# Token-side sums of an MLP block scheme in eight steps, and the second product's operands in the pairs' slots

## The chip, the cores and the metric

One core of a Trainium2 chip runs the whole kernel. The metric is the device time of one execution in microseconds; the time before is the median of three runs. Engines are called PE (matmul), DVE (VectorE), ACT (ScalarE) and SP, whose queue issues all the DMAs that matter here.

## The reference

One encoder block: a gated delta-rule mixer and a dilated attention mixer, gated, projected and added to x, then an MLP. The change lies in the MLP alone:

```python
    h2 = _rmsnorm(x, ln_mlp_pre[l])
    f = jnp.square(jax.nn.relu(jnp.einsum('bsd,df->bsf', h2, w_ff1[l])))
    f = jnp.einsum('bsf,fd->bsd', f, w_ff2[l])
    x = x + _rmsnorm(f, ln_mlp_post[l])
```

x is 1024 tokens by 1024 channels, w_ff1 1024 x 4096, w_ff2 4096 x 1024, all fp32.

## The kernel before

**Arithmetic.** Every fp32 operand X is split in two fp32r parts: `split` (L85 to L87) casts X to X_hi on ACT and subtracts on DVE, X_lo = X - X_hi. `mm3` (L108 to L112) makes one product of three matmuls, hi x hi, hi x lo, lo x hi. So each weight tile costs an ACT cast and a DVE subtraction before PE can finish with it. A weight tile is loaded to `w_raw` and split to `w_hi`, `w_lo`, with two buffers of each.

**Stages around the change.** `out_norm` writes the normalised, transposed MLP input for one half of the tokens (512) into `h_hi` and `h_lo`. While it does this for half 1, `build` issues plain tiles of the first product (`ff1_tile`) for columns c = 0 to 3 and half 0. Then `mlp` runs:

- `mid_blocks` (L998) adds and subtracts quarter blocks of `h` over the tokens' side: t1, and t2, t3, t4, which are split. It works on two channel pairs c = 0, 1; for each c there are 13 DVE operations of 128 x 1024 and three ACT casts. Temporaries have the tag "mid" (three buffers).
- plain tiles: c = 0 to 3 for half 1, then c = 4 and 5 for both halves. One half tile is 8 x 3 matmuls into one "mm" bank; ACT applies the ReLU (L958), DVE squares (L959), SP stores to `d_f` (L961).
- t1 is split into the place of the lower channel half of `h[1]` (called b12).
- `ff1_pair` (L1028) for c = 6, 8, ... 30: two column tiles at once with seven half-size products in place of eight. Their weight-side sums have the tag "mid"; products 1, 2, 4, 5, 6 take their operands from `x_hi`, `x_lo` (five buffers), products 0 and 3 from `w_hi`, `w_lo`. The last two DMAs of a pair store f1 (L1076) and f0 (L1083).
- both pools, "mid" and "midt" (t2 to t4), are closed, and pool "mlp" opens in their place. `ff2` (L963) makes the second product for each half of the tokens: for each of 32 blocks k it loads 128 rows of `d_f` to `f_raw` (L970), splits them to `f_hi`, `f_lo` (three buffers each), loads and splits 128 rows of `w_ff2`, and issues 24 matmuls into eight PSUM banks. Then it normalises and adds `fx`.

**Order.** The code is traced in the program's order; a planner then puts each engine's instructions into that engine's queue. It prefers work that is earlier in the program among what it holds ready, and gives an instruction its waits for data and for free buffers. On the chip each queue is worked off in order.

Of the kernel before, what the change touches and what calls it, by code (L numbers as in the profile page):

```python
# [10 lines left out]
F = mybir.dt.float32  # L11
R = mybir.dt.float32r
# [5 lines left out]
DM = 1024  # L18
# [52 lines left out]
class Kern:  # L71
# [888 lines left out]
        s = slice(512 * halves[0], 512 * halves[-1] + 512)  # L960
        nc.sync.dma_start(self.d_f[col:col + 128, s], f[:, s])  # L961

    def ff2(self, g, p, tmp):  # L963

        nc, a = self.nc, self.a
        bank = [("acc", 4)] * 4 + [("mm", self.mm_bufs)] * 2 + [("tr", 2)] * 2
        q = [self.pp.tile([128, 512], F, name=t, tag=t, bufs=n) for t, n in bank]
        for k in range(32):
            fr = p.tile([128, 512], F, name="f_raw", tag="f_raw", bufs=3)
            nc.sync.dma_start(fr, self.d_f[128 * k:128 * k + 128, 512 * g:512 * g + 512])  # L970
            W = self.wtile(a["w_ff2"][128 * k:128 * k + 128, :], [128, DM])
            f = [p.tile([128, 512], R, name=n, tag=n, bufs=3) for n in ("f_hi", "f_lo")]
            self.split(*f, fr)
            for t in range(4):
                for n in range(2):
                    self.mm3(q[2 * t + n], [x[:, 128 * t:128 * t + 128] for x in f],
                             [x[:, 512 * n:512 * n + 512] for x in W], k == 0, k == 31)
        xs, ys, sums = [], [], []
        for t in range(4):
            x = p.tile([128, DM], F, name="fx", tag="fx", bufs=4)  # L980
            nc.sync.dma_start(x, self.d_x1[512 * g + 128 * t:512 * g + 128 * t + 128, :])
            y = p.tile([128, DM], F, name="fy", tag="fy", bufs=4)
            ss = tmp.tile([128, 4], F, name="ss4", tag="ss4", bufs=12)
            for n in range(2):
                j = tmp.tile([128, 512], F, name="sj3", tag="ftmp", bufs=4)
                nc.scalar.activation(j, q[2 * t + n], AF.Square, accum_out=ss[:, n:n + 1])
                c = slice(512 * n, 512 * n + 512)
                nc.vector.tensor_tensor(y[:, c], q[2 * t + n], self.g_mlp[:, c], op=OP.mult)
            xs.append(x), ys.append(y), sums.append(ss)
        for t, (x, y, ss) in enumerate(zip(xs, ys, sums)):  # L990
            rows = slice(512 * g + 128 * t, 512 * g + 128 * t + 128)
            r = self.rms_of(tmp, ss[:, 0:2])
            for n in range(2):
                c = slice(512 * n, 512 * n + 512)
                nc.vector.scalar_tensor_tensor(y[:, c], y[:, c], r, x[:, c], op0=OP.mult, op1=OP.add)
                nc.sync.dma_start(a["out"][rows, c], y[:, c])

    def mid_blocks(self, h, pt, p):  # L998

        nc = self.nc  # L1000
        (H0, L0), (H1, L1) = h
        T = [[pt.tile([128, 4, 512], R, name=f"t{n}_{x}") for x in ("hi", "lo")] for n in (2, 3, 4)]
        t1 = p.tile([128, 4, 512], F, name="t1")
        new = lambda: p.tile([128, 2, 512], F, name="mid", tag="mid", bufs=3)
        add = lambda o, x, y: nc.vector.tensor_tensor(o, x, y, op=OP.add)
        sub = lambda o, x, y: nc.vector.tensor_tensor(o, x, y, op=OP.subtract)
        for c in range(2):
            u, v = slice(2 * c, 2 * c + 2), slice(4 + 2 * c, 6 + 2 * c)
            d = new()
            sub(t1[:, u], H1[:, u], H0[:, u])  # L1010
            sub(d, L1[:, u], L0[:, u])
            add(t1[:, u], t1[:, u], d)
            t3, d = new(), new()
            sub(t3, H1[:, v], H1[:, u])
            sub(d, L1[:, v], L1[:, u])
            add(t3, t3, d)
            self.split(T[1][0][:, u], T[1][1][:, u], t3)
            t2 = new()
            sub(t2, H1[:, v], t1[:, u])
            add(t2, t2, L1[:, v])  # L1020
            self.split(T[0][0][:, u], T[0][1][:, u], t2)
            t4 = new()
            sub(t4, H0[:, v], t2)
            add(t4, t4, L0[:, v])
            self.split(T[2][0][:, u], T[2][1][:, u], t4)
        return t1, T

    def ff1_pair(self, c, rhs, pf, p, tmp):  # L1028

# [53 lines left out]
        nc.sync.dma_start(self.d_f[128 * c:128 * c + 128], f0)  # L1083

    def mlp(self, h, pf, tmp):
        with ExitStack() as es:
            p = self.pool("mid", ctx=es)
            pt = self.pool("midt", ctx=es)
            t1, T = self.mid_blocks(h, pt, p)
            for c in range(4):  # L1090
                self.ff1_tile(c, h, (1,), pf)
            for c in range(4, 6):
                self.ff1_tile(c, h, (0, 1), pf)
            b12 = [x[:, 0:4] for x in h[1]]
            self.split(*b12, t1)
            rhs = dict(zip(("t2", "t3", "t4"), T), t1=b12, b11=[x[:, 0:4] for x in h[0]],
                       b21=[x[:, 4:8] for x in h[0]], b22=[x[:, 4:8] for x in h[1]])
            for c in range(6, 32, 2):
                self.ff1_pair(c, rhs, pf, p, tmp)
        p = self.pool("mlp")  # L1100
        self.g_mlp = self.row(p, "ln_mlp_post")
        for g in range(2):
            self.ff2(g, p, tmp)

    def row(self, p, name):
        t = p.tile([128, DM], F, name=name)
# [136 lines left out]
```

## Time and profile before

| | |
|---|---|
| median of 3 runs | 2261.99 us (2260.46 to 2264.52) |
| profiled execution | 2262.11 us, its span 2260.2 us |
| mean granted clock of PE | 0.988 |
| busy: PE, DVE, ACT | 97%, 64%, 34% of the span |
| the MLP's stages | plain tiles with sums to 1644, pairs to 1891, second product to 2248 |

Idle time counts where an engine on the chain that ended last stands still; PE makes 90% of that chain. In a row of a timeline the numbers are start and duration; in square brackets stand the idle time before and what ended it. Matmuls overlap: one of 512 columns lasts 0.39 us by its row and the next starts 0.23 us after it.

### The profile page before, as it was taken

Reading aid. Unit: us, or ns where it says so; the run is one execution under the profiler, and the core shown is the slowest. Engines: PE = TensorE matmul, PEld = TensorE weight load, DVE = VectorE, ACT = ScalarE, POOL = GpSimd, SP = SyncE. Lnnn points to the kernel's source line nnn. Section 1 sums busy time; section 2 is a strip of 40 time slices with the busy share of each in tenths; the row PEclk is TensorE's granted clock in tenths of the full one; section 3 lists DMA queues with packets and bytes.
Section 4 is the critical chain, followed back from the end, with each engine's and each line's share of the span. In section 5 each row is a group of like instructions: output and inputs, shape, how many; then the busy total and the mean of one; then the engine's idle time right before and its main releaser. Section 6 shows DMA issues by size and latency. Waiting matters only on the chain.

```text
span 2260.2 us, 30868 instructions
## 1 busy us (share of the span) xinstructions
PE 2192.2 (97%) x11763; PEld 1856.5 (82%) x11763; DVE 1435.9 (64%) x2538; ACT 779.6 (34%) x1663; POOL 61.4 (3%) x90
## 2 busy tenths in 40 slices
PE   7999999999999999999999999999799998999998
PEld 6887888879778878888888888988588887888886
DVE  5657563999599456777777755567656663335334
ACT  5334343333312323333333322434233332223322
POOL 0211211000000000000000000000000000000000
PEclk9999999999999999999999999999899999999999
DMA  5554755533732665444434257554233335445543
GB/s 176 174 166 136 221 156 158 162 113 102 173 86 71 176 195 159 116 117 117 117 117 117 91 192 249 174 178 142 85 107 112 112 112 181 149 140 173 195 144 107
DMA packets 300603, 326.05 MB, mean 144 GB/s; under 512 B 83012, under 2 KB 238620, under 8 KB 299432
## 3 DMA queue, kind: packets, MB, share of 16 engines
q1 hardware_dynamic: 300456, 324.09, 46.8%
q8 instruction: 92, 1.51, 0.3%
q14 instruction: 55, 0.45, 0.1%
HBM read 237.82 MB, written 89.37 MB: 145 GB/s over the span
## 4 chain that ended last, share of the span: by engine, by line
PE 90%; DVE 5%; ACT 2%; DMA 1%; issue 1%; SPq 0%; DVEq 0%; ACTq 0%
PE mm L112 15%; PE mm L110 15%; PE mm L111 15%; PE acc L1051 9%; PE acc L110 4%; PE acc L111 4%; PE acc L112 4%; PE tr L807 2%; PE gm L110 2%; PE gm L112 2%; PE gm L111 2%; PE ao L585 2%; PE mm L1051 2%; PE tr L110 1%; PE tr L112 1%; PE tr L111 1%
## 5 line engine op out<-in xcount | busy, mean ns | idle before, releaser
L110 PE MATMUL mm<-hT_hi,w_hi 128*128 128x512 f32 x960 | 391.0, 407 | 1.0 <-ACT xpad L335 0.6
L112 PE MATMUL mm<-hT_hi,w_lo 128*128 128x512 f32 x960 | 387.4, 404 | 1.3 <-DVE w_lo L87 1.2
L111 PE MATMUL mm<-hT_lo,w_hi 128*128 128x512 f32 x960 | 388.6, 405 | 0.0
L87 DVE TENSOR_TENSOR w_lo<-w_raw,w_hi 128x1024 fp32r<-128x1024 f32 (+1 forms) x225 | 260.7, 1159 | 148.3 <-ACT w_hi L86 146.4
L86 ACT CAST w_hi<-w_raw 128x1024 fp32r<-128x1024 f32 (+1 forms) x225 | 221.4, 985 | 335.5 <-PE mm L111 195.4
L112 PEld LDWEIGHTS mm<-hT_hi,w_lo 128*128 128x128 f32 x960 | 181.3, 189 | 34.7 <-DVE w_lo L87 3.5
L110 PEld LDWEIGHTS mm<-hT_hi,w_hi 128*128 128x128 f32 x960 | 181.4, 189 | 34.4 <-ACT vs L524 1.3
L111 PEld LDWEIGHTS mm<-hT_lo,w_hi 128*128 128x128 f32 x960 | 181.5, 189 | 31.2 <-issue 0.9
L87 DVE TENSOR_TENSOR f_lo<-f_raw,f_hi 128x512 fp32r<-128x512 f32 x64 | 44.2, 692 | 198.6 <-ACT f_hi L86 198.6
L340 DVE SCALAR_TENSOR_TENSOR cu<-xpad,conv,cu 128x1024 f32<-128x1024 f32 x96 | 125.4, 1307 | 3.3
L86 ACT CAST f_hi<-f_raw 128x512 fp32r<-128x512 f32 x64 | 39.9, 623 | 238.4 <-PE tr L111 225.3
L431 DVE TENSOR_TENSOR XA<-XB 128x62 f32<-128x62 f32 (+30 forms) x124 | 106.1, 856 | 20.5 <-ACT XB L427 17.7
L110 PE MATMUL mm<-w_hi,hT_hi 128*128 128x256 f32 x384 | 108.0, 282 | 0.3 <-ACT V L521 0.3
L434 DVE TENSOR_TENSOR XB<-XB,XA 128x62 f32<-128x62 f32 (+30 forms) x124 | 106.1, 856 | 3.0
L112 PE MATMUL mm<-w_hi,hT_lo 128*128 128x256 f32 x384 | 108.0, 282 | 0.0
L111 PE MATMUL mm<-w_lo,hT_hi 128*128 128x256 f32 x384 | 108.0, 282 | 0.0
L110 PE MATMUL acc<-w_hi,f_hi 128*128 128x512 f32 x256 | 100.8, 394 | 7.2 <-ACT f_hi L86 7.2
L111 PE MATMUL acc<-w_lo,f_hi 128*128 128x512 f32 x256 | 100.6, 393 | 0.0
L112 PE MATMUL acc<-w_hi,f_lo 128*128 128x512 f32 x256 | 100.6, 393 | 0.0
L110 PE MATMUL gm<-hT_hi,w_hi 128*128 128x512 f32 x208 | 83.5, 401 | 0.7 <-ACT bg L652 0.5
L576 ACT ACTIVATE P<-lg,st 128x256 f32<-128x256 f32 (+1 forms) x96 | 45.5, 474 | 109.9 <-DVE st L573 108.0
L112 PE MATMUL gm<-hT_hi,w_lo 128*128 128x512 f32 x208 | 81.9, 394 | 0.0
(336 smaller groups left out, 4932.7 us busy)
## 6 DMA issues: line engine op xcount, KB each, us to landing
w_raw<-in_w_ff SPq DMA_DIRECT2D x100, 512.0 KB
w_raw<-in_w_in SPq DMA_DIRECT2D x85, 512.0 KB
f_raw<-d_f SPq DMA_DIRECT2D x64, 256.0 KB
d_f<-f SPq DMA_DIRECT2D x28, 512.0 KB
d_g<-bg SPq DMA_DIRECT2D x32, 256.0 KB
G<-d_gcb SPq DMA_DIRECT2D x16, 512.0 KB
d_G<-G SPq DMA_DIRECT2D x16, 512.0 KB
E<-d_gcb SPq DMA_DIRECT2D x16, 512.0 KB
```

What stands on the lines that cost most here:

```text
L86: self.nc.scalar.copy(H, src)
L87: self.nc.vector.tensor_tensor(L, src, H, op=OP.subtract)
L110: t.matmul(p, lH, rH, start=first, stop=False)
L111: t.matmul(p, lH, rL, start=False, stop=False)
L112: t.matmul(p, lL, rH, start=False, stop=last)
L340: nc.vector.scalar_tensor_tensor(u, xp[:, t:t + S], cw[:, t:t + 1], u, op0=OP.mult, op1=OP.add)
L431: nc.vector.tensor_tensor(tv, XB[:, 0:j, j:j + 1].to_broadcast([128, j, n]), XB[:, j:j + 1, j + 1:64].to_broadcast([128, j, n]), op=OP.mult)
L434: nc.vector.tensor_tensor(dst, dst, tv, op=OP.add)
L576: nc.scalar.activation(P[:, 0:W], lg[:, 0:W], AF.Exp, bias=nm, scale=-1.0, accum_out=Z)
L585: nc.tensor.matmul(o[:, oc:oc + 128], V[:, kt], PT[:, 128 * n:128 * n + 128], start=n == 0, stop=n == len(keys) - 1)
L807: nc.tensor.matmul(o[:, t], x, y, start=i == 0, stop=i == len(mats) - 1)
L1051: nc.tensor.matmul(bank, X[x][:, k], r[y][:, k], start=start, stop=k == 3 and n == 2, skip_group_check=not first)
```

## The change

Two edits, both in the MLP.

1. `mid_blocks` becomes a generator. It hands out t1 and T first and then stops after each of eight steps (for each c: t1; t3; t2; t4). `mlp` asks for one step after each of the four half-1 tiles, and for two after each of the tiles c = 4 and 5. All operations stay.
2. Pool "mid" stays open to the end. In `ff2`, `f_raw` has the tag "mid", and `f_hi`, `f_lo` have the tags "x_hi", "x_lo" (five buffers). Only "midt" is closed; a pool "end" with the row `ln_mlp_post`, `fx` and `fy` takes its place.

```diff
-    def ff2(self, g, p, tmp):
+    def ff2(self, g, p, pe, tmp):
...
-            fr = p.tile([128, 512], F, name="f_raw", tag="f_raw", bufs=3)
+            fr = p.tile([128, 512], F, name="f_raw", tag="mid", bufs=3)
             nc.sync.dma_start(fr, self.d_f[128 * k:128 * k + 128, 512 * g:512 * g + 512])
             W = self.wtile(a["w_ff2"][128 * k:128 * k + 128, :], [128, DM])
-            f = [p.tile([128, 512], R, name=n, tag=n, bufs=3) for n in ("f_hi", "f_lo")]
+            f = [p.tile([128, 512], R, name=f"f_{n}", tag=f"x_{n}", bufs=5) for n in ("hi", "lo")]
             self.split(*f, fr)
...
-            x = p.tile([128, DM], F, name="fx", tag="fx", bufs=4)
+            x = pe.tile([128, DM], F, name="fx", tag="fx", bufs=4)
...
-            y = p.tile([128, DM], F, name="fy", tag="fy", bufs=4)
+            y = pe.tile([128, DM], F, name="fy", tag="fy", bufs=4)
...
+        yield t1, T
         for c in range(2):
...
             add(t1[:, u], t1[:, u], d)
+            yield
...
             self.split(T[1][0][:, u], T[1][1][:, u], t3)
+            yield
...
             self.split(T[0][0][:, u], T[0][1][:, u], t2)
+            yield
...
             self.split(T[2][0][:, u], T[2][1][:, u], t4)
-        return t1, T
+            yield
...
     def mlp(self, h, pf, tmp):
+        p = self.pool("mid")
         with ExitStack() as es:
-            p = self.pool("mid", ctx=es)
-            pt = self.pool("midt", ctx=es)
-            t1, T = self.mid_blocks(h, pt, p)
+            mid = self.mid_blocks(h, self.pool("midt", ctx=es), p)
+            t1, T = next(mid)
             for c in range(4):
                 self.ff1_tile(c, h, (1,), pf)
+                next(mid)
             for c in range(4, 6):
                 self.ff1_tile(c, h, (0, 1), pf)
+                next(mid), next(mid)
+            for _ in mid:
+                pass
...
-        p = self.pool("mlp")
-        self.g_mlp = self.row(p, "ln_mlp_post")
+        pe = self.pool("end")
+        self.g_mlp = self.row(pe, "ln_mlp_post")
         for g in range(2):
-            self.ff2(g, p, tmp)
+            self.ff2(g, p, pe, tmp)
```

## Rows read from the trace of the kernel before

**Rows 1.** The page, busy time of the engines (share of the span) and instructions

```profile
PE 2192.2 (97%) x11763; PEld 1856.5 (82%) x11763; DVE 1435.9 (64%) x2538; ACT 779.6 (34%) x1663; POOL 61.4 (3%) x90
```

**Rows 2.** Waits of PE, whole span: us in total, times, longest

```profile
PE mm L112 <- DVE w_lo L87: 19.8, 5, 17.9
...
PE acc L110 <- ACT f_hi L86: 7.2, 1, 7.2
```

**Rows 3.** Table by stage: stretch, length, busy by engine, granted clock, DMA share, GB/s

```profile
1580.00:1606.00 26.00, 7.95 (x24) 6.10 (x25) 24.88 (x23) 6.36 (x7) 0.00 (x0) 0.61 0.15 43
...
1893.00:1906.00 13.00, 7.43 (x22) 5.88 (x23) 2.03 (x3) 1.85 (x3) 0.00 (x0) 0.61 0.89 289
```

**Rows 4.** Timeline of PE, 1580 to 1604

```profile
1580.14 0.50 PE L110 MATMUL mm<-h_hi,w_hi 128*128 128x512 f32 x1 [0.95 <-ACT f L958]
1580.48 0.40 PE L111 MATMUL mm<-h_lo,w_hi 128*128 128x512 f32 x1
1598.78 0.79 PE L112 MATMUL mm<-h_hi,w_lo 128*128 128x512 f32 x1 [17.91 <-DVE w_lo L87]
...
1603.55 0.39 PE L111 MATMUL mm<-h_lo,w_hi 128*128 128x512 f32 x1
```

**Rows 5.** Timeline of DVE, 1571 to 1598

```profile
1571.81 1.22 DVE L1006 TENSOR_TENSOR t<-h_hi,h_hi 128x1024 f32<-128x1024 f32 x1
1572.94 0.68 DVE L87 TENSOR_TENSOR h_lo<-tr,h_hi 128x512 fp32r<-128x512 f32 x1
...
1576.47 1.22 DVE L1006 TENSOR_TENSOR mid<-h_hi 128x1024 f32<-128x1024 f32 x1
1577.61 1.22 DVE L1006 TENSOR_TENSOR mid<-h_lo 128x1024 f32<-128x1024 f32 x1
...
1597.51 1.21 DVE L87 TENSOR_TENSOR w_lo<-w_raw,w_hi 128x1024 fp32r<-128x1024 f32 x1
```

**Rows 6.** Timeline of ACT, 1573 to 1623

```profile
1573.15 1.06 ACT L86 CAST w_hi<-w_raw 128x1024 fp32r<-128x1024 f32 x1 [1.31 <-PE mm L111]
...
1579.50 0.59 ACT L958 ACTIVATE f<-mm 128x512 f32<-128x512 f32 x1
...
1617.42 0.59 ACT L958 ACTIVATE f<-mm 128x512 f32<-128x512 f32 x1
...
1622.86 0.59 ACT L958 ACTIVATE f<-mm 128x512 f32<-128x512 f32 x1
```

**Rows 7.** DVE's groups by line, 1571.8 to 1622.8: busy us, mean ns, idle before

```profile
L87 DVE TENSOR_TENSOR t_lo<-mid,t_hi 128x1024 fp32r<-128x1024 f32 x6 | 7.2, 1217 | 1.1 <-ACT t_hi L86 1.1
```

**Rows 8.** Chain that ended last, in order of time, 1892 to 1898

```profile
1892.76 0.33 SPq L1083
1893.13 4.69 DMA f_raw<-d_f
1897.90 0.63 ACT f_hi L86
```

**Rows 9.** Timeline of PE, 1890 to 1904

```profile
1890.98 0.39 PE L1051 MATMUL acc<-h_hi,x_lo 128*128 128x512 f32 x1
1898.57 0.79 PE L110 MATMUL acc<-w_hi,f_hi 128*128 128x512 f32 x1 [7.20 <-ACT f_hi L86]
...
1903.84 0.40 PE L110 MATMUL mm<-w_hi,f_hi 128*128 128x512 f32 x1
```

**Rows 10.** Timelines of ACT and then DVE, 1872 to 1884

```profile
1872.19 0.62 ACT L86 CAST x_hi<-mid 128x512 fp32r<-128x512 f32 x1 [2.09 <-PE acc L1051]
...
1877.81 0.59 ACT L1056 COPY keep<-acc 128x512 f32<-128x512 f32 x1 [1.37 <-PE acc L1051]
...
1883.31 0.69 DVE L1070 TENSOR_TENSOR f<-keep,acc 128x512 f32<-128x512 f32 x1 [6.09 <-PE acc L1051]
```

**Rows 11.** Timeline of ACT, 1629 to 1633

```profile
1629.56 0.62 ACT L86 CAST x_hi<-mid 128x512 fp32r<-128x512 f32 x1 [1.39 <-DVE mid L1037]
...
1632.42 0.62 ACT L86 CAST x_hi<-w_raw 128x512 fp32r<-128x512 f32 x1
```

## The prediction

> **What bounds the kernel now.** The page comes first: TensorE (PE) is busy for 97% of the span [rows 1], so time can only be won where PE stands still or runs slowly. The waits of PE over the whole span are read next. Nearly all of them are far from this change or under a microsecond, but two belong to the MLP, and each is a single long wait: 17.9 us for one `w_lo`, and 7.2 us for one `f_hi` [rows 2]. The table by stage then shows that each wait is followed by slow work: in 1580 to 1606 and in 1893 to 1906 the granted clock averages 0.61 [rows 3], that is, part of these stretches ran at 1.2 GHz, the lower level, after PE had stood idle.
>
> The timelines give the prices. A plain tile takes 5.44 us in the undisturbed stretch (from one evacuation to the next, 1617.42 to 1622.86, [rows 6]), and it has 8 x 3 = 24 matmuls, so the fast step is 5.44 / 24 = 0.227 us.
>
> *First wait.* PE begins tile c = 0 of token half 1, does two matmuls, and stops from 1580.48 to 1598.78 [rows 4]: 18.30 - 0.23 = 18.07 us lost. From 1598.78 to 1603.55 it makes 11 steps in 4.77 us, where fast ones take 2.50: 2.27 us more. Cause: this tile's `w_hi` was cast by 1574.2 [rows 6], but VectorE (DVE) starts its `w_lo` only at 1597.51 [rows 5]. In between DVE works through the sums of `mid_blocks` with hardly a pause, one 1024-wide operation every 1.135 us (1576.47, 1577.61). These sums come earlier in the program than the tile, and DVE prefers them whenever they are ready.
>
> *Second wait.* After the last matmul of the last pair (1890.98) the first matmul of `ff2` starts at 1898.57 [rows 9]: 7.59 - 0.23 = 7.36 us lost. From there to 1903.84 are 12 steps in 5.27 us instead of 2.72: 2.55 us more. The chain of waits names the cause: SP's queue issues the last store of `f` at 1892.76, the first `f_raw` load directly behind it at 1893.13, the load takes 4.69 us, and the cast follows [rows 8]. The load is of rows stored long before; what it waited for is memory, because pool "mlp" lies where the pairs' pool was.
>
> Together: 18.07 + 2.27 + 7.36 + 2.55 = 30.25 us.
>
> **The change part by part.**
>
> *Steps.* No operation is added or removed. The 26 wide DVE operations of `mid_blocks` (13 for each c) and six ScalarE casts keep their number; their place in the program moves behind tiles. Now `w_lo` of the first half-1 tile precedes step 1, that of the second precedes step 2, and so on. What a moved step issues is DVE and ScalarE work only; it has no DMA, so SP's queue is passed by nothing. That DVE is not bound to the program's order is shown by its timeline: the first sum runs at 1571.81, ahead of the `h_lo` at 1572.94 that belongs to the earlier `out_norm` [rows 5]. So I expect ready sums to keep filling DVE's idle time from 1571.8 on, and a ready `w_lo` to be taken at the next free slot, behind one running operation (1.1 us) and whatever DVE hasn't yet done of the steps ahead of it. The worst is c = 5, with steps 5 and 6 ahead (7 operations, 7.9 us, and its own 1.1); but its `w_hi` is ready 9.8 us before its matmuls (two half tiles less a cast).
>
> What hides the sums is 8 half tiles on PE. Without the stall PE reaches the half-1 tiles at 1580.14 - 0.95 = 1579.2 [rows 4] and the pairs at 1579.2 + 8 x 5.44 = 1622.7. From 1571.8 that is 50.9 us. DVE's work in it: 26 sums and 6 `w_lo`, 32 x 1.135 = 36.3; nine squares (two left of half 0, seven of these eight half tiles), one `h_lo` and the first pair's 10 pieces, all 512 wide at 0.605 (0.68 for one [rows 5], less the 0.08 by which successive ones overlap, as 1.22 against 1.135), 20 x 0.605 = 12.1. Sum 48.4 us of 50.9: it fits, with 2.5 us spare. Only one of the pair's ten pieces is needed at its start, so I charge nothing. If that cover were gone, the excess would reappear as a wait at the pairs' start.
>
> Here the Trainium skill speaks against the change: "VectorE: DVE Perf Modes" gives an fp32 two-input operation (N + 151) / 0.96 GHz (section on the TRN2 errata) and says that the next one doesn't start until the pipe is empty (section on the DRAIN). An estimate by that page is 32 x 1.224 + 20 x 0.691 = 53.0 us, 2.1 over, so the time would be up to 2.1 later. The trace agrees with the duration (1.22), but its starts are 1.135 apart; I go by the starts.
>
> The short 0.95 us wait at 1580.14, put down to the evacuation at 1579.50 [rows 4, 6], isn't addressed. It could go or stay, or a wait like it could be added at another boundary: bounds -0.95 and +0.95, value 0.
>
> *Slots.* `f_raw` takes a slot of "mid", `f_hi` and `f_lo` those of "x_hi" and "x_lo", and nothing of ff2's first operands waits for the pairs' pool to close. When are they free? The last split of the last pair is cast at 1872.19, and its `x_lo` ends by 1873.6, so all "mid" slots are free then; the first "x" slot goes with the product whose evacuation starts at 1877.81 [rows 10]. Ahead of the loads in the program stands the row load of `ln_mlp_post`, now in pool "end" on top of "midt": its last reader is the fourth product, ended by 1883.31 [rows 10]. Even if SP puts the `f_raw` load behind that row load, it issues by 1883.7, lands 4.7 later at 1888.4, and `f_hi` (0.67 to the start of PE) is ready at 1889.1, 2.1 us before PE needs it at 1891.2. So the wait and its slow clock vanish: 9.91 us. The four `fx` loads (0.5 MB each) move ahead with "end". They could only delay loads for later k; their cost lies between 0 and the 4.69 of one load [rows 8], and I take 0, since k = 3 is needed three tiles (16 us) later.
>
> Could `ff2` steal slots from the pairs? In the stretch before the first pair, the cast of `x_hi` straight from `w_raw` (fifth in the program's order) runs at 1632.42, after that from `mid` at 1629.56, for which ScalarE idled 1.39 us [rows 11], although the sum in that `mid` reads the same weight tile. That reads as slots handed out in the program's order, so I cost this at nothing.
>
> Sum: the profiled execution took 2262.1 (span 2260.2 and 1.9 around it), within 0.1 of the median of the three runs. 2262.1 - 30.25 = **2231.9**; own range 2229 to 2236 (0.95 either way, the page's 2.1, small waits).
>
> **The rivals.**
>
> *DVE fills up.* Each of the six `t_lo` waits for its cast on ScalarE, and once before DVE idled 1.1 us for it [rows 7]. If all six do, 48.4 + 6.6 = 55.0, that is 4.1 us over; PE then waits and slows (2.27): 2231.9 + 6.4 = 2238.3. Against it: during 1571.8 to 1597 other ready sums nearly always filled such waits. Chance 0.08.
>
> *The loads stay late.* If SP's order puts `f_raw` behind the store of f1 or f0, whose data come from the last pair's squares, the second wait stays in part or whole: 2231.9 + (2.6 + 2.5, from a load issued at 1888.4) = 2237, to 2231.9 + 9.91 = 2241.8. For it: SP takes its queue in order, and [rows 8] show just this line-up. Against it: the loads are ready 10 us before those stores. Chance 0.10.
>
> *The steps don't change DVE's order.* If the order was set by when operations are ready and `w_lo` counts as late, the first stall stays: 2262.1 - 9.9 = 2252.2. Against it: `w_hi` was done at 1574.2. Chance 0.05; for neither part working, 2262, 0.02.
>
> *Slower: the steps stand in DVE's queue in the program's order.* Then at each tile's end comes the evacuation (0.59), the square (0.61), the step (3 operations, 3.4 us, or 4, 4.5) and only then the next `w_lo` (1.13), while PE has 0.45 us of matmuls that don't need it. The first four boundaries cost 5.3 + 6.4 + 5.3 + 5.3, that with seven operations 9.8, the last (six, and a 512-wide `w_lo`) 8.2: 40.3 us, with 2.3 us of slow clock after each 54: 2231.9 + 54 = 2286. It makes the kernel slower once six boundaries lose over 5.0 us each. The engine's queue is first in, first out by the Trainium skill ("TensorE: Matmul & The Clock Gate", row on queue depth), which the late `w_lo` agrees with. Against this rival stands the sum at 1571.81 ahead of earlier work [rows 5]. Chance 0.05.
>
> **How the numbers follow.** Forecast 0.70, rivals as above. Range 2228 to 2242: the forecast's own 2229 to 2236, a microsecond below, and the first two rivals up to 2241.8; together 0.88, and cutting off the second would leave out too much. Two tenths of a per cent (4.5 us) is about what a measurement of this kernel can tell from no change. Faster by more: 0.70 + 0.08 + 0.10 + 0.05 = 0.93. Within: 0.02. Slower: 0.05.
>
> **What would show it.** Right: PE's waits no longer hold the two long rows; the granted clock is 1.00 throughout 1580 to 1630; `w_lo` of the first half-1 tile starts within 2 us of its `w_hi`, with sums spread between later ones; the first `f_raw` is issued before the last pair's stores; `ff2`'s first matmul follows the last pair's within 0.5 us, near 1871. Wrong: a new DVE wait at the start of the pairs or at tile boundaries, idle time of DVE before `t_lo`, or waits within the pairs, which had none.

## The result, and the profile after

The changed kernel takes 2231.13 us (median of four, 2227.34 to 2232.79), the kernel before 2262.89 beside it. The ratio is 0.9858, with a 95% interval of 0.9841 to 0.9875: about 32 us faster. The forecast was 2231.9. The profiled execution took 2232.79, with a span of 2231.0, so the two traces to be compared differ by 29.2 us in span. One later execution of the changed kernel, the profiled one beside the kernel with three buffers for `xr` below, took 9735.5 us; its trace isn't read, and it counts in no ratio.

First the waits of PE from 1500 us to the end (us in total, times, longest). The two long waits of [rows 2] are gone. Of the row for `w_lo` 2.4 us are left, nearly all of it one wait of 2.3 us near 1567 us, and the 0.95 us of [rows 4] is gone too.

```profile
PE mm L112 <- DVE w_lo L87: 2.4, 2, 2.3
PE mm L110 <- ACT w_hi L86: 0.2, 1, 0.2
```

Then the table by stage (length, busy by engine, granted clock, DMA share, GB/s). In 1580 to 1606, where [rows 3] show 7.95 us of PE and 0.61, PE is busy all the time at a clock of 1.00; so it is in 1871 to 1884, which now holds the start of `ff2`. The stage before, 1551 to 1580, holds the wait of 2.3 us and has 0.94.

```profile
1551.00:1580.00 29.00, 26.35 (x120) 20.71 (x119) 24.61 (x45) 14.34 (x32) 0.00 (x0) 0.94 0.61 191
1580.00:1606.00 26.00, 26.00 (x117) 21.52 (x116) 25.97 (x26) 10.67 (x13) 0.00 (x0) 1.00 0.46 142
...
1871.00:1884.00 13.00, 13.00 (x59) 10.78 (x58) 4.07 (x6) 3.97 (x6) 0.00 (x0) 1.00 0.86 289
```

DVE's timeline answers to [rows 5]. The `w_lo` at 1577.60 is that of the first half-1 tile; its `w_hi` was cast from 1575.41 to 1576.46. In [rows 5, 6] the same pair of operations lay 23 us apart. The next `w_lo` follows at 1582.14, after three sums, and so on. The last sums end at 1616.9, and the first pair's pieces at 1622.9.

```profile
1575.81 1.21 DVE L1008 TENSOR_TENSOR mid<-h_lo,h_lo 128x1024 f32<-128x1024 f32 x1
1576.99 0.69 DVE L959 TENSOR_TENSOR f<-f 128x512 f32<-128x512 f32 x1
1577.60 1.22 DVE L87 TENSOR_TENSOR w_lo<-w_raw,w_hi 128x1024 fp32r<-128x1024 f32 x1
1578.73 1.22 DVE L1007 TENSOR_TENSOR t<-t,mid 128x1024 f32<-128x1024 f32 x1
1579.87 1.22 DVE L1008 TENSOR_TENSOR mid<-h_hi 128x1024 f32<-128x1024 f32 x1
1581.00 1.22 DVE L1008 TENSOR_TENSOR mid<-h_lo 128x1024 f32<-128x1024 f32 x1
1582.14 1.22 DVE L87 TENSOR_TENSOR w_lo<-w_raw,w_hi 128x1024 fp32r<-128x1024 f32 x1
...
1615.66 1.22 DVE L87 TENSOR_TENSOR t_lo<-mid,t_hi 128x1024 fp32r<-128x1024 f32 x1
...
1622.21 0.68 DVE L87 TENSOR_TENSOR x_lo<-mid,x_hi 128x512 fp32r<-128x512 f32 x1
1623.78 2.29 DVE L87 TENSOR_TENSOR h_lo<-t,h_hi 128x2048 fp32r<-128x2048 f32 x1 [0.88 <-ACT h_hi L86]
```

At the second place, SP's timeline shows the first `f_raw` load at 1848.74, and loads on both sides of the last pair's stores (1869.11 and 1873.82) where [rows 8] have them behind the last store.

```profile
1848.74 0.32 SPq L970 DMA_DIRECT2D f_raw<-d_f  x1
...
1863.90 0.33 SPq L1118 DMA_DIRECT2D ln_mlp_post<-in_ln_mlp_post  x1
1864.29 0.43 SPq L981 DMA_DIRECT2D fx<-d_x  x1
...
1869.11 0.32 SPq L1082 DMA_DIRECT2D d_f<-f  x1
...
1873.82 0.32 SPq L1089 DMA_DIRECT2D d_f<-f  x1
```

And PE's timeline there, in place of [rows 9]: the first matmul of `ff2` follows the last one of the pairs 0.23 us later, at full speed.

```profile
1871.64 0.39 PE L1057 MATMUL acc<-h_hi,x_lo 128*128 128x512 f32 x1
1871.87 0.39 PE L110 MATMUL acc<-w_hi,f_hi 128*128 128x512 f32 x1
1872.10 0.39 PE L111 MATMUL acc<-w_lo,f_hi 128*128 128x512 f32 x1
```

**Where the 29.2 us went.** Four marks cut both traces (before, then after): the evacuation of the last half-0 tile starts at 1579.50 and 1581.76; the pairs at 1643.69 and 1624.35; `ff2` at 1898.57 and 1871.87; the last matmul at 2249.07 and 2219.80.

| Stretch | before | after | difference | forecast |
|---|---|---|---|---|
| to the end of half 0's tiles | 1579.50 | 1581.76 | +2.26 | 0 |
| half-1 and later plain tiles | 64.19 | 42.59 | -21.60 | -20.34 |
| pairs and the step to `ff2` | 254.88 | 247.52 | -7.36 | -7.36 |
| `ff2` to the last matmul | 350.50 | 347.93 | -2.57 | -2.55 |

The +2.26 lies ahead of the changed code. There, in this execution, a load of x for `out_norm` came late. DVE waited 1.44 us for it, the `w_lo` that a tile needed stood behind its consumers on DVE, and PE stood still for 2.26 us (0.9 in the trace before) and then made six slow steps. DVE's row and then PE's:

```profile
1564.18 1.28 DVE L932 SCALAR_TENSOR_TENSOR xr<-y,r,xr 128x1024 f32<-128x1024 f32 x1 [1.44 <-DMA xr<-in_x]
```

```profile
1567.85 0.79 PE L112 MATMUL mm<-h_hi,w_lo 128*128 128x512 f32 x1 [2.26 <-DVE w_lo L87]
1568.44 0.63 PE L110 MATMUL mm<-h_hi,w_hi 128*128 128x512 f32 x1
1568.87 0.63 PE L111 MATMUL mm<-h_lo,w_hi 128*128 128x512 f32 x1
...
1571.01 0.44 PE L110 MATMUL mm<-h_hi,w_hi 128*128 128x512 f32 x1
```

### The profile page after: what moved, and what is told of

Read it like the earlier page. It is cut to its first block, busy times and chain, and to the rows that moved or that the text cites. A ratio compares the mean times of both kernels' runs of the same rounds, so it can differ in the third digit from the quotient of the medians.

```text
span 2231.0 us, 30874 instructions
## 1 busy us (share of the span) xinstructions
PE 2188.4 (98%) x11763; PEld 1854.1 (83%) x11763; DVE 1433.1 (64%) x2538; ACT 778.6 (35%) x1663; POOL 63.0 (3%) x90
## 4 chain that ended last, share of the span: by engine, by line
PE 89%; DVE 4%; DMA 2%; ACT 2%; issue 1%; SPq 0%; POOL 0%; DVEq 0%; ACTq 0%; POOLq 0%
PE mm L112 15%; PE mm L110 14%; PE mm L111 14%; PE acc L1057 10%; PE acc L110 4%; PE acc L111 4%; PE acc L112 4%; PE gm L110 2%; PE tr L807 2%; PE gm L112 2%; PE gm L111 2%; PE ao L585 2%; PE mm L1057 2%; PE tr L110 1%; PE tr L111 1%; PE tr L112 1%
```

## Experiments

The theory: 20.3 us (with the 0.95 us wait 21.3) come from the steps and 9.9 from the slots, independently; the steps work because DVE prefers what is early in the program among what is ready, and the slots because `f_raw` had waited for memory. The rivals are those of the prediction. Medians stand beside those of the kernel before on the same chip; ratios are to that kernel. Edits are shown against the changed kernel, and three dots mark what is left out of them.

**The changed kernel again.**

> The changed kernel again, beside the others of this group. Theory (two stalls removed: 20.3 us from the steps with their slow clock, 9.9 from the slots): about 31 us under the kernel before, 2228 to 2234. It also tells whether the 2.3 us wait at 1567 us, which the first trace of the changed kernel shows behind a late xr load and a slow clock after it, is there in every execution: if it comes and goes, spans differ by 2 to 5 us with it.

2232.51 us against 2263.91, ratio 0.9863 (0.9845 to 0.9881). In this execution the wait near 1567 us was 0.7 us, with no slow clock (1551 to 1580 at 1.00), so the 2.3 us come and go. Its span is 2230.7 all the same, so a few microseconds come and go in earlier stages too.

**Steps alone.** `ff2` and its pool as before:

```diff
-            fr = p.tile([128, 512], F, name="f_raw", tag="mid", bufs=3)
+            fr = p.tile([128, 512], F, name="f_raw", tag="f_raw", bufs=3)
...
-        pe = self.pool("end")
+        p = self.pool("mlp")
```

> Only the steps; ff2 keeps its own buffers in pool mlp. Theory: the first stall goes (18.07 + 2.27, and the 0.95 at the boundary), the second stays with 7.4 us and its slow clock: 2262.5 - 21 = 2241.5, between 2239 and 2244. Rival (the two edits need each other, or the steps only move the wait to the pairs' start): above 2250.

2240.21 us, ratio 0.9899 (0.9878 to 0.9921). Of the two long waits only the second is left; waits of PE from 1500 us on:

```profile
PE acc L110 <- ACT f_hi L86: 6.7, 1, 6.7
PE mm L112 <- DVE w_lo L87: 1.1, 2, 0.9
```

SP's timeline shows that the order of [rows 8] is still there, the load right behind the last store:

```profile
1868.59 0.33 SPq L1118 DMA_DIRECT2D ln_mlp_post<-in_ln_mlp_post  x1
1869.94 0.33 SPq L1089 DMA_DIRECT2D d_f<-f  x1
1870.32 1.94 SPq L970 DMA_DIRECT2D f_raw<-d_f  x3
```

The row load of `ln_mlp_post`, which goes into the same pool as `f_raw`, is issued at 1868.59, as the last matmul of the pairs ends. So, as far as the rows show, the load of `f_raw` waited for memory until about then, and the rest of the 1.7 us up to 1870.32 for its place in SP's queue behind the store. In the trace before the same two loads lie 1.7 us apart too, at 1891.40 and 1893.13.

**Slots alone.** The sums are drawn before the first half-1 tile:

```diff
             t1, T = next(mid)
+            for _ in mid:
+                pass
             for c in range(4):
                 self.ff1_tile(c, h, (1,), pf)
-                next(mid)
...
-                next(mid), next(mid)
-            for _ in mid:
-                pass
```

> Only the slots; all sums come before the half-1 tiles as before. Theory: the second stall goes (7.36 + 2.55), the first stays: 2262.5 - 9.9 = 2252.6, between 2251 and 2255. Rival (loads stay late without the steps): 2262.

2252.78 us, ratio 0.9951 (0.9936 to 0.9966), 0.2 from the expected value. The first wait is back with its old size, and with it the 1.0 us wait for an evacuation:

```profile
PE mm L112 <- DVE w_lo L87: 18.8, 3, 17.9
PE mm L110 <- ACT f L958: 1.0, 1, 1.0
```

The two parts alone give 23.7 and 11.1 us against the common 2263.91, the whole 31.4; the ratios' intervals are wide enough for parts that simply add up (1.0 and 0.5% against 1.4%).

**All sums behind the first half-1 tile.**

```diff
                 self.ff1_tile(c, h, (1,), pf)
-                next(mid)
+                if c == 0:
+                    for _ in mid:
+                        pass
...
-                next(mid), next(mid)
-            for _ in mid:
-                pass
```

> Both edits, but all 26 sums stand behind the first half-1 tile instead of in eight steps. Theory (DVE prefers what comes earlier in the program among what is ready, so the second tile's w_lo waits for the sums): the first stall moves one tile later, from 5 us shorter than before to as long: PE waits 12 to 18 us for w_lo of tile c = 1 and then runs slowly for 2.3 us, 2245 to 2252. Rival (it is enough that the first tile has its weights; the number of steps does nothing): as the changed kernel, 2231.

2250.11 us, ratio 0.9935 (0.9919 to 0.9952). The wait has moved one tile on. PE's timeline, and then DVE's `w_lo` of the second tile, whose `w_hi` was done at 1582.5 (1581.44 and 1.06 on ScalarE):

```profile
1588.52 0.50 PE L110 MATMUL mm<-h_hi,w_hi 128*128 128x512 f32 x1 [1.00 <-ACT f L958]
1603.40 0.80 PE L112 MATMUL mm<-h_hi,w_lo 128*128 128x512 f32 x1 [14.15 <-DVE w_lo L87]
```

```profile
1602.13 1.22 DVE L87 TENSOR_TENSOR w_lo<-w_raw,w_hi 128x1024 fp32r<-128x1024 f32 x1
```

A ready `w_lo` stood 19.6 us behind sums that are earlier in the program. So it isn't enough that the first tile has its weights.

**All sums behind the last plain tile, no steps.**

```diff
                 self.ff1_tile(c, h, (1,), pf)
-                next(mid)
             for c in range(4, 6):
                 self.ff1_tile(c, h, (0, 1), pf)
-                next(mid), next(mid)
             for _ in mid:
                 pass
```

> Both edits, but no steps: all 26 sums stand behind the last plain tile. Theory (what matters is only that a ready w_lo stands ahead of the sums; ready sums fill DVE's idle time wherever they stand): first sum still at about 1572 to 1574 us, no wait of PE, same time as the changed kernel, ratio 0.984 to 0.988. Rival (the spreading itself is needed, since sums that come last are also done last): a wait at the start of the pairs, 5 us or more above the changed kernel.

2233.41 us, ratio 0.9869 (0.9856 to 0.9883): not to be told from the changed kernel. The first sum still starts at 1574.38, before the first half-1 tile, though in the program all sums now stand behind the plain tiles, and the last one ends at 1617.3, about as with the steps:

```profile
1574.38 1.22 DVE L1008 TENSOR_TENSOR t<-h_hi,h_hi 128x1024 f32<-128x1024 f32 x1
...
1616.06 1.23 DVE L87 TENSOR_TENSOR t_lo<-mid,t_hi 128x1024 fp32r<-128x1024 f32 x1
```

So eight steps aren't needed. What counts is that no long block of sums stands ahead of a `w_lo` in the program: all 26 cost 14 to 18 us of waiting, the three or four of a step none. With all sums behind the tiles the planner spreads them by itself.

**`f_raw` in pool "end".**

```diff
-            fr = p.tile([128, 512], F, name="f_raw", tag="mid", bufs=3)
+            fr = pe.tile([128, 512], F, name="f_raw", tag="f_raw", bufs=3)
```

> As the changed kernel, but f_raw has buffers of its own in pool end (on top of midt) instead of the slots of mid. Theory (the load waited for memory, and midt is free 8 us before the end of the last pair): loads are issued at about 1864 instead of 1849, land by 1869, the cast is ready about 2 us before PE needs it: same time, ratio 0.984 to 0.989. Rival (the loads get behind the stores of the last pair or share the DMA engines with the fx loads): PE waits 2 to 7 us for f_hi and then runs slowly, 2236 to 2242.

2232.56 us, ratio 0.9864 (0.985 to 0.9877), no wait at `ff2`. This is the order that the prediction took as its worst case (loads behind the row load). The lines are from SP's, ScalarE's and PE's timelines, a fence each:

```profile
1865.07 0.33 SPq L1118 DMA_DIRECT2D ln_mlp_post<-in_ln_mlp_post  x1
1865.44 1.37 SPq L970 DMA_DIRECT2D f_raw<-d_f  x3
```

```profile
1870.25 1.96 ACT L86 CAST f_hi<-f_raw 128x512 fp32r<-128x512 f32 x3 [1.87 <-DMA f_raw<-d_f]
```

```profile
1873.03 0.39 PE L110 MATMUL acc<-w_hi,f_hi 128*128 128x512 f32 x1
```

From issue to cast are 4.8 us, and with 0.67 for the cast the operand is ready 2.1 us before PE uses it, the very margin of the prediction. So the load needed free memory early, not the slots of "mid" in particular.

**Six and thirteen more sums.** The sums added write to a tile of their own that nothing reads, (3, 3) and (7, 6) for the two c:

```diff
+        spare = pt.tile([128, 2, 512], F, name="spare")
...
+            for _ in range((3, 3)[c]):
+                sub(spare, H1[:, v], H0[:, v])
             sub(t4, H0[:, v], t2)
```

> As the changed kernel, with six more sums of 1024 columns (three in each fourth step of a c), whose results nothing reads. Theory (DVE has 2.5 us spare before the pairs, and 9 of the first pair's 10 pieces, 5.4 us, may come later): 6 x 1.135 = 6.8 us are still covered; 0 to 1 us slower than the changed kernel, no wait of over 1 us at the pairs' start. Rival (DVE is full already, as its timeline without idle time suggests): 7 us and a slow clock, 9 us slower.

> As the changed kernel, with 13 more sums (seven and six), whose results nothing reads. Theory: 14.8 us against 2.5 + 5.4 of cover, so PE waits about 6.9 us in the first pair and then runs slowly for 2.3: 7 to 11 us slower than the changed kernel. Rival (DVE full): 14.8 + 2.3 = 17 us slower. Rival (sums are hidden further on in the pairs, where DVE is 60% busy): nothing.

With six, 2234.55 us, ratio 0.9875 (0.9859 to 0.9891); with thirteen, 2246.03, ratio 0.9928 (0.9914 to 0.9942). PE's waits from 1550 us on, first with six, then with thirteen:

```profile
PE acc L1060 <- DVE x_lo L87: 1.6, 1, 1.6
```

```profile
PE acc L1060 <- ACT x_hi L86: 9.4, 1, 9.4
```

6.8 us of extra work cost 1.6 us of waiting, and 14.8 cost 9.4, 0.8 more at a tile boundary, and then slow steps (in 1630 to 1650 the clock averages 0.74). PE's timeline with thirteen shows both waits:

```profile
1604.06 0.50 PE L112 MATMUL mm<-h_hi,w_lo 128*128 128x512 f32 x1 [0.83 <-DVE w_lo L87]
...
1635.51 0.79 PE L1060 MATMUL acc<-t_hi,x_hi 128*128 128x512 f32 x1 [9.39 <-ACT x_hi L86]
```

So 5.2 and 4.6 us were covered, against 2.5 + 5.4 = 7.9 expected, and both expectations were missed: with six the wait is over the 1 us allowed for, and with thirteen the time is about 14 us above the changed kernel's, not 7 to 11. One thing that was missing is the split of t1, which is earlier in the program than the pair's pieces and takes DVE 2.2 us in the same place; DVE's timeline with thirteen:

```profile
1629.64 1.22 DVE L1008 TENSOR_TENSOR spare<-h_hi,h_hi 128x1024 f32<-128x1024 f32 x1
1630.78 2.28 DVE L87 TENSOR_TENSOR h_lo<-t,h_hi 128x2048 fp32r<-128x2048 f32 x1
1632.98 1.22 DVE L1008 TENSOR_TENSOR spare<-h_hi,h_hi 128x1024 f32<-128x1024 f32 x1
1634.12 0.68 DVE L1046 TENSOR_TENSOR mid<-w_raw 128x512 f32<-128x512 f32 x1
```

That leaves 7.9 - 2.2 = 5.7. With thirteen, the rows give the rest: DVE also makes a tenth square ahead of the first piece (0.6 us), the cast of that piece lies between DVE and PE (0.8 us, from the next start on DVE at 1634.72 to 1635.51), and PE makes two matmuls of the pair before it waits (0.5 us): 5.7 - 0.6 - 0.8 + 0.5 = 4.8. With six, PE waits for the fifth piece and not for the first, after 14 matmuls of the pair, so that its 5.2 us follow from another sum, which isn't worked out here. The rival by which DVE has no room at all (7 and 14.8 us of wait) falls, and so does the one by which the pairs hide everything.

**Three buffers for `xr`,** to look at what is left before the pairs, with the changed kernel beside it:

```diff
-            x = p.tile([128, DM], F, name="xr", tag="xr", bufs=2)
+            x = p.tile([128, DM], F, name="xr", tag="xr", bufs=3)
```

> As the changed kernel, but out_norm has three buffers for xr instead of two, so the third load of x in each half no longer waits for a buffer. Theory (what is left before the pairs is the load of xr: it landed 6.7 us after its issue in the first trace of the changed kernel, w_lo stood behind its consumer on DVE, PE waited 2.3 us and ran slowly for 3 us, but 0.7 us without slow clock in other traces): the wait at 1567 to 1571 goes, 0.7 to 3.5 us faster than the changed kernel, ratio 0.9845 to 0.986. Rival (the wait is the order of DVE's work and not the load): the 0.7 us stay, no difference.

> The changed kernel beside it on the same chip: ratio 0.985 to 0.988, and a look at whether its wait at 1567 to 1571 us is 0.7 or 2.3 us in this execution.

2232.2 us, ratio 0.9859 (0.9844 to 0.9873), against 0.9856 (0.9839 to 0.9872) for the changed kernel: no difference. What the wait was in the changed kernel beside it isn't known. With three buffers PE's longest wait from 1500 us on is still 0.7 us for a `w_lo`, although no load of xr is late here: the tile's `w_hi` was done at 1564.5, and its `w_lo` starts only at 1567.91, behind operations of `out_norm`. So the 0.7 us come from the order of DVE's work, as the rival had it. Whether a third buffer would prevent the 2.3 us, which showed in two traces of these kernels (the first of the changed kernel, and that with all sums behind the first tile), stays open: the late load didn't occur where it could have been compared.

## Why the prediction was right, point by point

**The two prices.** Both stalls were read as start-to-start distances plus the slow steps behind them, and the table of four marks gives them back: 7.36 against 7.36 for the wait at `ff2`, 2.57 against 2.55 for its slow clock. For the first stall it is 21.60 against 20.34. That the median lies within 0.8 us of the forecast is in part luck: the executions scatter over 5 us, and in the profiled one the 1.26 us gained beyond the price at the first stall and the 2.26 us lost ahead of it partly cancel.

**The short wait at the boundary (value 0, bounds of 0.95 either way).** It went, and with it 0.95 of the 1.26 us by which the first stall's gain exceeds its price. The runs show more than the prediction saw: the wait is in every kernel in which PE waits over 14 us for a `w_lo` (before, slots alone, all sums behind the first tile) and in none of the others. It went with the stall; why the bank was given out so that the tile waited isn't shown.

**The steps.** That DVE takes ready sums early and a ready `w_lo` before later sums is what its timeline shows. The prediction let each step follow a tile, as the change does; the run with all sums behind the plain tiles shows that the eight steps aren't needed for it, only that the block doesn't stand ahead of the `w_lo`.

**The cover.** 48.4 us of DVE work were reckoned into 50.9. In the trace after DVE works from 1573.46 to 1622.9 with under 0.3 us of idle time. It began 1.7 us later than reckoned because of the late x load, and so did the pairs (1624.35 against 1622.7). The sum by starts 1.135 and 0.605 us apart holds: 32 operations of 1024 columns and 21 of 512 (ten pieces, nine squares, two `h_lo`) give 49.0 us for these 49.4. By the Trainium skill ("VectorE: DVE Perf Modes", the sections on the errata and on the DRAIN), the same work is an estimated 32 x 1.224 + 21 x 0.691 = 53.7 us; the measurement decides for the starts. In its section on the DRAIN the Trainium skill adds that an operation which isn't held starts earlier, which the estimate in the prediction had left out; the rows agree, with starts 1.135 us apart at 1.22 us long. The prediction's own slip is the split of t1: its 2.2 us on DVE come at the pairs' start and belong into the sum of what must be done there. By the two runs with more sums the change has about 5 us of cover (5.2 and 4.6) rather than the 7.9 that follow from the prediction's terms. Since the change adds no work, the slip cost nothing.

**The slots.** Right in time, and in mechanism but for one part: the prediction laid the load's wait to memory alone, and the last 1.4 us or so of it were its place behind the store in SP's queue (1.7 us after the row load, where 0.4 us lie between the two with `f_raw` in "end"). Free memory removed both, since the load then went ahead of the store. The worst case of the prediction was built (`f_raw` in "end") and its margin of 2.1 us measured. The `fx` loads, moved ahead to 1864 and after, cost nothing visible: PE is busy throughout 1871 to 1884 with a DMA share of 0.86, and its waits show no row from 1571 us to the end.

**What wasn't foreseen** is the late x load ahead of the changed code, +2.26 us in the profiled execution. It lies in the scatter of this kernel (2227 to 2233) and isn't an effect of the change: from 1302 to 1577 us the rows of DVE, ACT and SP stand in the same order in both traces.

**The rivals.** The wait at the pairs' start appears only when sums are added (1.6 us with six). The loads behind the stores appear with the steps alone. The strict program order on DVE (2286) is excluded by the run with all sums last, where a sum that stands behind all plain tiles in the program starts before the half-1 tiles. That the steps don't change DVE's order (2252) is excluded by the `w_lo` at 1577.60. That waits for `t_lo` fill DVE up (2238) is excluded by its timeline, which has under 0.3 us of idle time in this stretch.

## What to carry to other kernels

Where a planner prefers early work, a block of preparation that is ready at once and needed late belongs behind the work that feeds PE, in the program; here idle time then took it up, and finer steps added nothing. A wait at the seam of two stages may be for memory and for the queue behind it: look at what is queued just ahead of the first load, and give the load space that is free earlier. When work is to be hidden, count everything on that engine which must come before the first consumer, and test the cover by adding dummy work until a wait appears.

## What the runs showed of the hardware

In these traces short waits of PE came without slow steps, longer ones with them: after 1.61 us (six more sums, PE starts again at 1628.78) the granted clock stayed 1.00 in 1606 to 1630 and in 1630 to 1650, and after 2.26 us (first trace after) six steps were about 0.43 us apart before 0.23 returned. The slow steps need not come at once: after 2.29 us (all sums behind the first tile) PE made steps of about 0.23 us up to 1569.40 and only then, from 1569.69 to 1572.67, seven of about 0.43 us.

DVE's two-input fp32 operations overlap: 1.22 us long and 1.135 us apart at 1024 columns, 0.69 and 0.605 at 512. Where the second reads what the first has just written, they don't: 1.25 us apart (1590.16 and 1591.41 in the trace after) and 0.72 (1883.31 and 1884.03 before).

The same load of x (0.5 MB) reached its consumer 6.8 us after its issue in the first trace after (1557.37 to 1564.18), issued behind two weight loads as in the trace before, and PE waited 2.3 us for what stood behind it. In the trace before its consumer ran 5.5 us after the issue (1557.93 to 1563.42) without waiting for it. In all the traces but these two, the first after and that with all sums behind the first tile, PE's wait at that place was 0.7 to 0.9 us.
